# One tile distance in each stage, and w_out tiles split two units ahead, in an fp32 hybrid encoder layer

## The chip, the cores and the metric

The kernel runs on one core of a Trainium2 chip. The metric is the time of one execution on the device in microseconds, as the median of several runs. The chip's engines that matter here are PE (TensorE: matmuls, and the loads of their stationary operand), DVE (VectorE), ACT (ScalarE), POOL (GpSimd) and SP (SyncE, which here only issues DMAs).

## The reference

One encoder layer on x of 256 positions by 2048 channels, batch 1, everything in float32:

```python
xn = _rmsnorm(h, pre_mix_gain[l])
proj = xn @ w_in[l]                       # 2048 x 3904: hyena x0, x1, v | latents of the attention
xh = _dwconv_centred(xh, hyena_conv_w[l], hyena_conv_b[l])
y_hyena = x0 * _bidir_long_conv(x1 * v, k2, hyena_bias[l])
y_attn = _mla(c_q, c_kv, k_pe, ...)       # 8 heads, softmax over 256 keys
mixed = concatenate([_rmsnorm(y_hyena), _rmsnorm(y_attn)]) @ w_out[l]     # 2048 x 2048
h = h + _rmsnorm(mixed, post_mix_gain[l])
hn = _rmsnorm(h, pre_ffn_gain[l])
gu = hn @ w_up[l]                         # 2048 x 11264
g = _dwconv_centred(gu[..., :D_FF], ffn_conv_w[l], ffn_conv_b[l])
f = (gelu(g) * gu[..., D_FF:]) @ w_down[l]    # 5632 x 2048
h = h + _rmsnorm(f, post_ffn_gain[l])
```

## The kernel before

Every weight is read once from memory, in units of 128 x 1024 floats (512 KB). `load` (L131) issues the DMA on SP's queue into a `raw` tile. `split_w` makes two tiles of it: a high part `wh`, a cast to the rounded format fp32r on ACT (L140), and a low part `wl`, the rest, as a subtraction on DVE (L143). `raw`, `wh` and `wl` come from the pool `wp` with four buffers each, so a unit's load waits until the unit four before it has been split, and a split waits until PE is done with the unit four before. The activations are split in the same way. PE then multiplies high by high, high by low and low by high.

PE's stages, in the order of the program:

- The input's norm and the attention's latents.
- The hyena projection: 24 half outputs `hi` of two units each (`why...`, L113 to L115, three matmuls of 256 columns for each of 16 k). The weights are the stationary operand, the activations `xT` move. Attention and the long convolution run between them as generators in the list `chains`; `turn()` takes each one step further after every unit. `hyena_tail` finishes a half output: `z` (L616), then the three taps of the convolution (`cv`, L551 and L553).
- The output projection (`wo`, L100 to L102): `row_units` runs over two halves of 16 units (`w_out00` to `w_out015`, `w_out10` to `w_out115`). Here the activations `mix[k]` are stationary and the weights move, 512 columns at a time; a unit is 12 matmuls (two row blocks, two column blocks, three products). `row_units` stages one unit ahead of the one that PE uses. During the first eight units the last steps of the chains still run: `channel_norm` scales and splits `ya` and `yh` into `mix` on DVE (L763 and L92), with the row scale spread over partitions by a matmul (`rbh`, L161). The rest of the row vectors follow: `gbm` and `gbn` (two gain vectors, spread over 128 partitions, 1 MB each) and `h` (x, two loads of 1 MB) are loaded through POOL's queue (L873 to L877).
- Norms and the first tile of the up projection, whose weights have a pool of their own (`up0`).
- The up projection (`pg` and `pu`, `wmm`, L108 and L109): 43 more tiles of four units each. The weights are stationary. For each of 16 k, and for `pg` and `pu`, one matmul of 512 columns with the high weights and one of 256 columns with the low weights, a pair; 32 pairs a tile. `up_tail` makes the gated result `fT[n]`.
- The down projection (`wd`, also L100 to L102): two halves of 44 units, `fT[k]` stationary, weights moving; then the last norm and the output.

PE loads the stationary operand of the next matmul while the present one runs. Where the two tiles lie in SBUF is set by the pools: `W_SLOT = 1024 + 16` floats makes each of the four slots of `wh` and `wl` begin 64 bytes further than the last, counted modulo 256 bytes, so that the four units in use begin at 0, 64, 128 and 192. `xT` and `hnT` begin at 0, `mix` at 128; `fT` has a pad of 16 floats after every four tiles, so that it steps by 64 bytes too. The order of the work on each engine is that of the code, except where `tc.issue_after` puts an instruction behind a named one.

Of the kernel before, what the change touches and what calls it, by code (L numbers as in the profile page):

```python
# [12 lines left out]
F32 = mybir.dt.float32  # L13
F32R = mybir.dt.float32r
# [4 lines left out]
P = 128  # L19
D = 2048  # L20
S = 256
KD = D // P
# [6 lines left out]
NF = DFF // P  # L29
# [20 lines left out]
V_FCB = 274  # L50
V_ALL = 318
V_PAD = 320
W_SLOT = 1024 + 16


def _body(ctx, tc, a):
    nc = tc.nc
# [6 lines left out]

    const = ctx.enter_context(tc.tile_pool(name="const", bufs=1))
    edge = ctx.enter_context(tc.tile_pool(name="edge", bufs=1, side="right"))
    edge.tile([P, 24], F32, name="edge")
    wp = ctx.enter_context(tc.tile_pool(name="wp", bufs=4))
    psA = ctx.enter_context(tc.tile_pool(name="psA", bufs=2, space=bass.MemoryType.PSUM))
    psB = ctx.enter_context(tc.tile_pool(name="psB", bufs=3, space=bass.MemoryType.PSUM))  # L70
# [59 lines left out]

    def load(src, n, name):  # L131
        raw = wp.tile([P, 1024], F32, tag="raw", name=name)
        nc.sync.dma_start(raw[:, :n], src)
        return raw

    def split_w(raw, n, name, pool=None, cut=None):
        pool = pool or wp
        h = pool.tile([P, W_SLOT], F32R, tag="wh", name=name + "h")
        l = pool.tile([P, W_SLOT], F32R, tag="wl", name=name + "l")
        box["cast"] = nc.scalar.copy(h[:, :n], raw[:, :n])  # L140
        for e, o in ((nc.vector, slice(0, cut or n)), (nc.gpsimd, slice(cut or n, n))):
            if o.start < n:
                box["lo"] = e.tensor_tensor(l[:, o], raw[:, o], h[:, o].bitcast(F32), op=ALU.subtract)  # L143
        return h, l

    def stage(src, n, name, pool=None, cut=None):

        return split_w(load(src, n, name), n, name, pool, cut)

    def rms_scale(ss, n, name, pool, bufs=4):  # L150
        v = small(pool, 1, tag="rv", name=name + "v", bufs=bufs)
# [14 lines left out]
    box = {}  # L166
# [13 lines left out]
    yp = l_stack.enter_context(tc.tile_pool(name="yp", bufs=1, side="left"))  # L180
    spec = l_stack.enter_context(tc.tile_pool(name="spec", bufs=1, side="left"))
    xTp = l_stack.enter_context(tc.tile_pool(name="xTp", bufs=1, side="left"))
    xT = [xTp.tile([P, 2, 2, P], F32R, name=f"xT{k}") for k in range(KD)]
    ya = [yp.tile([P, S], F32, name=f"ya{i}") for i in range(8)]
    yh = [yp.tile([P, S], F32, name=f"yh{i}") for i in range(8)]
# [15 lines left out]
    x = a["x"]  # L201
# [114 lines left out]
    for k in range(KD):  # L316
# [7 lines left out]
        wh, wl = wm[k]  # L324
# [445 lines left out]
    def attention_chain():  # L770
        nonlocal mixp, mix
        yield from latents()
        yield from attention()
        yield from pause(2)
        at_stack.close()
        mixp = mix_stack.enter_context(tc.tile_pool(name="mixp", bufs=1, side="right"))
        mix = [mixp.tile([P, 2, S], F32R, name=f"mix{k}") for k in range(KD)]
        yield from channel_norm(sqa, ya, V_AG, mix[0:8], "a", mi)

    mixp = mix = None  # L780
# [3 lines left out]
    next(att)  # L784
    order = [(0, 0), (0, 1), (1, 0), (0, 2), (1, 1), (2, 0),
             (2, 1), (1, 2), (3, 0), (3, 1), (2, 2), (3, 2)]
    for i, gi in order:
        for c in range(2):
            ps = (acc if cv else mj)(f"hi{i}{gi}{c}")[:, :S]
            for kh in range(2):  # L790
                wh, wl = stage(a["w_hy"][i, gi, c, kh], 1024, f"why{i}{gi}{c}{kh}")
                for kk in range(8):
                    k = kh * 8 + kk
                    wm3(ps, wh[:, kk * P : (kk + 1) * P], wl[:, kk * P : (kk + 1) * P], xT[k],
                        k == 0, k == KD - 1)
                if kh == 1:
                    if not cv:
                        row_scale_tile()
                    hyena_tail(i, gi, c, ps)
                turn()  # L800

    def row_units(wname, nk, half, lT, ps, hold, held):
        def get(k):
            return stage(a[wname][half, k], 1024, f"{wname}{half}{k}")

        nxt = get(0)
        for k in range(nk):
            w, nxt = nxt, get(k + 1) if k + 1 < nk else None
            for b in range(2):
                if b == 1 and k >= nk - hold:  # L810
                    held.append((k, w))
                    continue
                for c in range(2):
                    row_emit(ps[b][c], lT, k, b, w, c, nk)
            yield
# [35 lines left out]
        return rms_scale(ss, n, nm, pool)  # L851

    psw = row_banks(0, "wo0")
    units = row_units("w_out", KD, 0, mix, psw, 0, None)
    for _ in range(8):
        next(units)
        turn()
# [5 lines left out]
    h = [hp.tile([P, D], F32, name=f"h{b}") for b in range(2)]  # L863
    rb2 = hp.tile([P, S], F32, name="rb2")
    hn_stack = es()
    hnp = hn_stack.enter_context(tc.tile_pool(name="hnp", bufs=1, side="left"))
    hnTq = [hnp.tile([P, 4, 2, 2, P], F32R, name=f"hnT{c}") for c in range(4)]
    hnT = [hnTq[k // 4][:, k % 4] for k in range(KD)]
    pm_stack = es()
    pm = pm_stack.enter_context(tc.tile_pool(name="pm", bufs=1, side="left"))  # L870
    up0 = pm_stack.enter_context(tc.tile_pool(name="up0", bufs=4, side="left"))
    gbm = pm.tile([P, D], F32, name="gbm")
    nc.gpsimd.dma_start(gbm, a["post_mix_gain"].partition_broadcast(P))  # L873
    gbn = pm.tile([P, D], F32, name="gbn")
    nc.gpsimd.dma_start(gbn, a["pre_ffn_gain"].partition_broadcast(P))
    for b in range(2):
        nc.gpsimd.dma_start(h[b], x[b * P : (b + 1) * P, :])  # L877
    tmp = [pm.tile([P, D], F32, name=f"tmp{b}") for b in range(2)]
    ssq = [small(pm, 4, name=f"ssq{b}") for b in range(2)]
    ss2 = [small(pm, 4, name=f"ss2{b}") for b in range(2)]  # L880
    for _ in units:
        pass
    for b in range(2):
        for c in range(2):
            row_finish(psw, 0, b, c, gbm, tmp, ssq, pm)
# [26 lines left out]
    held = []  # L912
    psw = row_banks(1, "wo1")
    for k, _ in enumerate(row_units("w_out", KD, 1, mix, psw, HOLD, held)):
        if k == KD - HOLD - 2:
            first = [stage(a["w_up"][0, kq], 1024, f"wup0{kq}", up0) for kq in range(4)]
    row_finish(psw, 1, 0, 0, gbm, tmp, ssq, pm)
# [12 lines left out]
    fq = fpa_stack.enter_context(tc.tile_pool(name="fq", bufs=2, side="right"))  # L930
    fpa = fpa_stack.enter_context(tc.tile_pool(name="fpa", bufs=1, side="right"))
    NFA = 12
    def gated_tiles(pool, ks):
        for k in ks:
            if k % 4 == 0:
                pool.tile([P, 16], F32, name=f"fpad{k}")
            yield pool.tile([P, 2, S], F32R, name=f"fT{k}")

    fT = list(gated_tiles(fpa, range(NFA)))

    def up_tail(n, pg, pu):

# [49 lines left out]
    for n in range(1, NF):  # L992
        if n == 4:
            fpb = fpa_stack.enter_context(tc.tile_pool(name="fpb", bufs=1, side="right"))
            fT += gated_tiles(fpb, range(NFA, NF))
        new = (mi, mj) if n % 2 else (acc, acc)
        pg, pu = as4(new[0](f"pg{n}")), as4(new[1](f"pu{n}"))
        chs = []
        for kq in range(4):
            with es() as hold:  # L1000
                if n == 1:
                    for eng in range(2):
                        hold.enter_context(tc.issue_after(box[int(kq >= 2), 3, eng].ins))
                chs.append(stage(a["w_up"][n, kq], 1024, f"wup{n}{kq}"))
        for which, ps in ((0, pg), (1, pu)):
            for k in range(KD):
                wh, wl = chs[k // 4]
                o = (k % 4) * 256 + which * P
                wmm(ps, wh[:, o : o + P], wl[:, o : o + P], hnT[k], k == 0, k == KD - 1)
        up_tail(n, pg, pu)  # L1010
# [16 lines left out]
    for half in range(2):  # L1027
        psd = row_banks(half, f"wd{half}")
        held = []
# [117 lines left out]
```

## Time and profile before

| | |
|---|---|
| time, median of 3 runs | 1115.65 us (1114.95 to 1116.01) |
| the profiled execution | 1114.86 us |
| its span | 1113.1 us |
| PE busy | 1096.4 us, 99% |
| DVE, ACT, POOL busy | 65%, 52%, 11% |
| hyena projection, attention, long convolution | about 46 to 259 us |
| output projection | 259 to 352 us |
| norms, first tile of the up projection | 352 to 378 us |
| up projection, 43 tiles | 378 to 860 us |
| down projection | 860 to 1098 us |

The span is the time from the first to the last instruction of the profiled execution; some 2 us lie around it. PE's share of 99% says how long matmuls were running, not how fast they followed one another: the timeline of single matmuls tells that, from the start of one to the start of the next (a matmul's own duration there is longer than the spacing, since matmuls are pipelined). The mean of a group is taken from two rows far apart and the count of matmuls between them.

### The profile page before, as it was taken

To read this page: it belongs to the slowest core of one execution; us is meant where nothing else is said; L and a number is where in the kernel's file an instruction comes from. 1 tells how busy PE (TensorE), PEld (TensorE's weight loads), DVE (VectorE), ACT (ScalarE), POOL (GpSimd) and SP (SyncE) were. 2 spreads that over 40 slices of the span, in tenths; PEclk is the share of its full clock that TensorE was granted. 3 is DMA by queue.
4 is the path that set the end of the run, shared out by engine and by line. 5 is a ranking of instruction groups with operands and counts; after the bars stand their busy time and mean duration, and the time that the engine had idled before them with its cause. 6 is when DMAs were issued, how large, how long until landed. Compare 5 with 4: busy or idle time off the path is not lost.

```text
span 1113.1 us, 16496 instructions
## 1 busy us (share of the span) xinstructions
PE 1096.4 (99%) x6334; PEld 959.4 (86%) x6334; DVE 725.8 (65%) x1051; ACT 574.3 (52%) x884; POOL 122.3 (11%) x154
## 2 busy tenths in 40 slices
PE   9999999999999999999999999999999999999997
PEld 7899999998787888888888888888888888888885
DVE  7898878889567766666666666565756444454444
ACT  7756656655454646454545455554545333343332
POOL 4300100011002311111111111111111000000000
PEclk9999999999999999999999999999999999999999
DMA  9664445444775354645464645555555766666652
GB/s 312 224 212 148 161 133 171 143 136 131 276 253 189 114 190 162 216 157 219 156 214 164 204 176 197 182 188 191 179 199 172 258 188 191 189 192 188 189 191 95
DMA packets 59207, 207.23 MB, mean 186 GB/s; under 512 B 6903, under 2 KB 7801, under 8 KB 58489
## 3 DMA queue, kind: packets, MB, share of 16 engines
q1 hardware_dynamic: 57832, 200.39, 54.1%
q0 software_dynamic: 720, 5.24, 1.3%
q8 instruction: 49, 0.80, 0.3%
q10 hardware_dynamic: 576, 0.56, 0.1%
q14 instruction: 30, 0.24, 0.1%
HBM read 204.07 MB, written 2.10 MB: 185 GB/s over the span
## 4 chain that ended last, share of the span: by engine, by line
PE 86%; issue 6%; DVE 5%; DMA 1%; POOL 1%; ACT 1%; DVEq 0%; POOLq 0%; SPq 0%; ACTq 0%
PE pg L108 14%; PE pu L108 14%; PE pg L109 7%; PE pu L109 7%; PE wd L102 7%; PE wd L100 7%; PE wd L101 7%; PE hi L113 4%; PE hi L115 4%; PE hi L114 4%; DMA w_out<-in_w_out 1%; POOL tmp L893 1%; PE y L499 1%; PE pq L101 1%; PE pq L100 1%
## 5 line engine op out<-in xcount | busy, mean ns | idle before, releaser
L91 ACT CAST fT<-u 128x256 fp32r<-128x256 f32 x44 | 17.8, 406 | 111.1 <-DVE u L952 111.0
L551 DVE SCALAR_TENSOR_TENSOR t<-g,vec,t 128x255 f32<-128x255 f32 x44 | 21.3, 483 | 63.8 <-ACT t L550 63.8
L948 POOL TENSOR_TENSOR u<-u,rb 128x256 f32<-128x256 f32 x44 | 32.4, 736 | 276.4 <-DVE u L125 276.4
L550 ACT ACTIVATE t<-g,vec 128x256 f32<-128x256 f32 x44 | 26.5, 603 | 54.9 <-POOL g L946 54.9
L125 DVE TENSOR_TENSOR g<-pg,jg 128x256 f32<-128x256 f32 x44 | 18.7, 424 | 52.5 <-ACT jg L124 52.5
L946 POOL TENSOR_TENSOR g<-g,rb 128x256 f32<-128x256 f32 x44 | 32.4, 736 | 137.6 <-DVE g L125 136.2
L124 ACT COPY jg<-pg 128x256 f32<-128x256 f32 x44 | 16.3, 371 | 54.7 <-PE pg L109 54.7
L952 DVE TENSOR_TENSOR u<-u,t 128x256 f32<-128x256 f32 x44 | 18.7, 424 | 36.4 <-POOL u L948 35.4
L834 POOL TENSOR_TENSOR rw0r<-rw0v,neghalf 128x1 f32<-128x1 f32 x2 | 1.1, 558 | 292.1 <-DVE rw0v L831 292.1
L92 DVE TENSOR_TENSOR fT<-u,fT 128x256 fp32r<-128x256 f32 x44 | 18.7, 425 | 19.8 <-ACT fT L91 19.8
L553 DVE SCALAR_TENSOR_TENSOR t<-g,vec,t 128x255 f32<-128x255 f32 x44 | 21.3, 484 | 1.5
L547 POOL TENSOR_TENSOR sqa<-sqa,sqa 128x256 f32<-128x256 f32 x7 | 6.8, 965 | 128.9 <-ACT sqa L546 128.6
L951 ACT ACTIVATE t<-t 128x256 f32<-128x256 f32 x44 | 18.2, 414 | 2.7 <-DVE t L553 2.7
L125 DVE TENSOR_TENSOR u<-pu,ju 128x256 f32<-128x256 f32 x44 | 18.3, 417 | 0.0
L550 ACT ACTIVATE cv<-z,vec 128x256 f32<-128x256 f32 x24 | 14.4, 601 | 7.5 <-DVE z L616 7.5
L232 POOL TENSOR_TENSOR sqx<-sqx,sqx 128x256 f32<-128x256 f32 x15 | 15.7, 1047 | 17.8 <-ACT sqx L231 17.6
L124 ACT COPY ju<-pu 128x256 f32<-128x256 f32 x44 | 16.0, 364 | 0.0
L96 DVE SCALAR_TENSOR_TENSOR xT<-xraw,vec,xT 128x256 fp32r<-128x256 f32 x16 | 11.8, 740 | 2.7 <-ACT xT L95 2.7
L893 POOL TENSOR_TENSOR tmp<-h,gbn 128x512 f32<-128x512 f32 x8 | 13.3, 1682 | 2.4 <-DVE h L890 2.4
L616 DVE TENSOR_TENSOR z<-hi,rbx 128x256 f32<-128x256 f32 x24 | 10.0, 418 | 5.2 <-PE hi L115 4.9
L547 POOL TENSOR_TENSOR sqh<-sqh,sqh 128x256 f32<-128x256 f32 x7 | 7.8, 1114 | 47.6 <-ACT sqh L546 47.5
L553 DVE SCALAR_TENSOR_TENSOR cv<-z,vec,cv 128x255 f32<-128x255 f32 x24 | 12.4, 518 | 0.2
(3679 smaller groups left out, 4378.0 us busy)
## 6 DMA issues: line engine op xcount, KB each, us to landing
wup<-in_w_up SPq DMA_DIRECT2D x176, 512.0 KB, 4.8
w_down<-in_w_down SPq DMA_DIRECT2D x88, 512.0 KB, 3.5
why<-in_w_hy SPq DMA_DIRECT2D x48, 512.0 KB, 3.9
w_out<-in_w_out SPq DMA_DIRECT2D x32, 512.0 KB, 4.3
wm<-in_w_mla SPq DMA_DIRECT2D x16, 416.0 KB, 4.9
win<-in_window SPq DMA_DIRECT2D x8, 256.0 KB, 3.1
wuq<-in_w_uqn SPq DMA_DIRECT2D x4, 512.0 KB, 3.5
wkv<-in_w_ukv SPq DMA_DIRECT2D x4, 512.0 KB, 4.1
```

The source lines that it names most:

```text
L100: ins = nc.tensor.matmul(ps, lhsT=lh, rhs=rh, start=first, stop=False)
L101: nc.tensor.matmul(ps, lhsT=lh, rhs=rl, start=False, stop=False)
L102: nc.tensor.matmul(ps, lhsT=ll, rhs=rh, start=False, stop=last)
L108: nc.tensor.matmul(ps, lhsT=wh, rhs=xt, start=first, stop=False)
L109: nc.tensor.matmul(ps[:, :, 0, :], lhsT=wl, rhs=xt[:, :, 0, :], start=False, stop=last)
L113: nc.tensor.matmul(ps, lhsT=wh, rhs=xt[:, :, 0, :], start=first, stop=False)
L114: nc.tensor.matmul(ps, lhsT=wh, rhs=xt[:, :, 1, :], start=False, stop=False)
L115: box["mm"] = nc.tensor.matmul(ps, lhsT=wl, rhs=xt[:, :, 0, :], start=False, stop=last)
L125: nc.vector.tensor_add(d, ps4[:, :, 0, :], lo)
L550: nc.scalar.activation(dst, src, AF.Identity, bias=vc(bv), scale=vc(wv + 1))
L553: nc.vector.scalar_tensor_tensor(dst[:, : S - 1], src[:, 1:], vc(wv + 2), dst[:, : S - 1], op0=ALU.mult, op1=ALU.add)
L946: nc.gpsimd.tensor_tensor(g, g, rb2, op=ALU.mult)
```

## The change

There are three parts.

1. The layout. `W_SLOT` goes: all four slots of `wh` and of `wl` begin at the same place modulo 256 bytes. `wl` gets 64 floats more, so that a low tile can be put `o` floats further; the up projection's 43 tiles use `o=16`, 64 bytes. New pads move `xT` and `hnT` to 64 and `mix` to 0; the pads within `fT` go and it lies at 0. The address of the stationary tile less that of the moving one, modulo 256, becomes 192 in the hyena projection, 0 in the output and down projections, and in the up projection 192 for the high and 0 for the low weights. Before, it ran through 0, 64, 128 and 192 in each of them.
2. `row_units` keeps two units staged ahead, and the first two units of `w_out` are staged in the last half output of the hyena projection (`got`).
3. `gbm`, `h` and `gbn` are no longer loaded in four pieces of 1 MB through POOL's queue; twelve pieces go through SP's, each behind the load of one unit (`piece`): four of `gbm` behind `w_out010` to `w_out013`, four of `h` (512 KB) behind `w_out11` to `w_out14`, four of `gbn` behind `w_out15` to `w_out18`.

```diff
-W_SLOT = 1024 + 16
-    edge.tile([P, 24], F32, name="edge")
+    edge.tile([P, 40], F32, name="edge")
...
-        nc.sync.dma_start(raw[:, :n], src)
+        box["load"] = nc.sync.dma_start(raw[:, :n], src)
...
-    def split_w(raw, n, name, pool=None, cut=None):
+    def split_w(raw, n, name, pool=None, cut=None, o=0):
+
         pool = pool or wp
-        h = pool.tile([P, W_SLOT], F32R, tag="wh", name=name + "h")
-        l = pool.tile([P, W_SLOT], F32R, tag="wl", name=name + "l")
+        h = pool.tile([P, 1024], F32R, tag="wh", name=name + "h")
+        l = pool.tile([P, 1024 + 64], F32R, tag="wl", name=name + "l")[:, o : o + 1024]
...
+    xTp.tile([P, 16], F32, name="xpad")
     xT = [xTp.tile([P, 2, 2, P], F32R, name=f"xT{k}") for k in range(KD)]
...
         mix = [mixp.tile([P, 2, S], F32R, name=f"mix{k}") for k in range(KD)]
+        mixp.tile([P, 16], F32, name="mpad")
...
+    got = []
     for i, gi in order:
...
+                if (i, gi, c) == (3, 2, 1):
+                    got.append(stage(a["w_out"][0, kh], 1024, f"w_out0{kh}"))
...
-    def row_units(wname, nk, half, lT, ps, hold, held):
+    def row_units(wname, nk, half, lT, ps, hold, held, got=()):
...
-        nxt = get(0)
+        ws = list(got) or [get(0)]
         for k in range(nk):
-            w, nxt = nxt, get(k + 1) if k + 1 < nk else None
+            if len(ws) < nk:
+                ws.append(get(len(ws)))
+            w = ws[k]
...
+    hnp.tile([P, 16], F32, name="hpad")
...
-    nc.gpsimd.dma_start(gbm, a["post_mix_gain"].partition_broadcast(P))
...
-    nc.gpsimd.dma_start(gbn, a["pre_ffn_gain"].partition_broadcast(P))
-    for b in range(2):
-        nc.gpsimd.dma_start(h[b], x[b * P : (b + 1) * P, :])
+
+    def piece(dst, src, c, n):
+
+        o = slice(c * n, (c + 1) * n)
+        with tc.issue_after(box["load"].ins):
+            nc.sync.dma_start(dst[:, o], src[:, o])
+
...
-    for _ in units:
-        pass
+    for k, _ in enumerate(units):
+        if k < 4:
+            piece(gbm, a["post_mix_gain"].partition_broadcast(P), k, 512)
...
+        if k < 4:
+            piece(h[k // 2], x[k // 2 * P : (k // 2 + 1) * P, :], k % 2, 1024)
+        elif k < 8:
+            piece(gbn, a["pre_ffn_gain"].partition_broadcast(P), k - 4, 512)
...
-    def gated_tiles(pool, ks):
-        for k in ks:
-            if k % 4 == 0:
-                pool.tile([P, 16], F32, name=f"fpad{k}")
-            yield pool.tile([P, 2, S], F32R, name=f"fT{k}")
-
-    fT = list(gated_tiles(fpa, range(NFA)))
+    fT = [fpa.tile([P, 2, S], F32R, name=f"fT{k}") for k in range(NFA)]
+    fpa.tile([P, 16], F32, name="fpad")
...
-                chs.append(stage(a["w_up"][n, kq], 1024, f"wup{n}{kq}"))
+                chs.append(stage(a["w_up"][n, kq], 1024, f"wup{n}{kq}", o=16))
```

What stands on DVE at the end of the hyena projection, before. `z321` and `cv321` are the last half output's tail, `ya` and `mix` the attention's part of the output projection's stationary operand, `w_out01l` the low part of the second unit:

```order
L616 TENSOR_TENSOR z321_3587<-hi321_3520,rbx_125 128x256
L763 SCALAR_TENSOR_TENSOR ya4_111<-ya4_111,vec_74,rba_3238 128x256
L763 SCALAR_TENSOR_TENSOR ya5_112<-ya5_112,vec_74,rba_3238 128x256
L551 SCALAR_TENSOR_TENSOR cv321_3589<-z321_3587,vec_74,cv321_3589 128x255
L92 TENSOR_TENSOR mix4_3226<-ya4_111,mix4_3226 128x256
L553 SCALAR_TENSOR_TENSOR cv321_3589<-z321_3587,vec_74,cv321_3589 128x255
L92 TENSOR_TENSOR mix5_3227<-ya5_112,mix5_3227 128x256
L143 TENSOR_TENSOR w_out01l_3612<-w_out01_3609,w_out01h_3611 128x1024
L763 SCALAR_TENSOR_TENSOR ya6_113<-ya6_113,vec_74,rba_3238 128x256
L763 SCALAR_TENSOR_TENSOR ya7_114<-ya7_114,vec_74,rba_3238 128x256
L143 TENSOR_TENSOR w_out02l_3651<-w_out02_3648,w_out02h_3650 128x1024
```

The same place on DVE in the changed kernel:

```order
L143 TENSOR_TENSOR w_out01l_3598<-w_out01_3595,w_out01h_3597 128x1024
L617 TENSOR_TENSOR z321_3601<-hi321_3522,rbx_126 128x256
L764 SCALAR_TENSOR_TENSOR ya4_112<-ya4_112,vec_74,rba_3240 128x256
L764 SCALAR_TENSOR_TENSOR ya5_113<-ya5_113,vec_74,rba_3240 128x256
L552 SCALAR_TENSOR_TENSOR cv321_3603<-z321_3601,vec_74,cv321_3603 128x255
L91 TENSOR_TENSOR mix4_3227<-ya4_112,mix4_3227 128x256
L554 SCALAR_TENSOR_TENSOR cv321_3603<-z321_3601,vec_74,cv321_3603 128x255
L143 TENSOR_TENSOR w_out02l_3620<-w_out02_3617,w_out02h_3619 128x1024
L91 TENSOR_TENSOR mix5_3228<-ya5_113,mix5_3228 128x256
L764 SCALAR_TENSOR_TENSOR ya6_114<-ya6_114,vec_74,rba_3240 128x256
L764 SCALAR_TENSOR_TENSOR ya7_115<-ya7_115,vec_74,rba_3240 128x256
```

`w_out01l` now stands ahead of `z321`, and `w_out02l` ahead of `mix5`.

SP's queue in the second part of the first half of `w_out`, before (`w_out09` to `w_out014` are the units' loads):

```order
L133 DMA w_out09_3866<-in_w_out 128x1024
L133 DMA w_out010_3884<-in_w_out 128x1024
L133 DMA w_out011_3902<-in_w_out 128x1024
L133 DMA w_out012_3920<-in_w_out 128x1024
L133 DMA w_out013_3938<-in_w_out 128x1024
L133 DMA w_out014_3956<-in_w_out 128x1024
```

And in the changed kernel:

```order
L132 DMA w_out09_3821<-in_w_out 128x1024
L132 DMA w_out010_3871<-in_w_out 128x1024
L887 DMA gbm_3863<-in_post_mix_gain 128x512
L132 DMA w_out011_3890<-in_w_out 128x1024
L887 DMA gbm_3863<-in_post_mix_gain 128x512
L132 DMA w_out012_3909<-in_w_out 128x1024
L887 DMA gbm_3863<-in_post_mix_gain 128x512
L132 DMA w_out013_3928<-in_w_out 128x1024
L887 DMA gbm_3863<-in_post_mix_gain 128x512
L132 DMA w_out014_3947<-in_w_out 128x1024
```

The four quarters of `gbm`, which was one issue on POOL, stand each behind one unit's load.

## Rows read from the trace of the kernel before

**Rows 1.** The page's busy time of each engine, share of the span, instructions.

```profile
PE 1096.4 (99%) x6334; PEld 959.4 (86%) x6334; DVE 725.8 (65%) x1051; ACT 574.3 (52%) x884; POOL 122.3 (11%) x154
```

**Rows 2.** Timeline of PE, hyena projection: start, duration, line, operation, tiles, shapes.

```profile
204.19 0.28 PE L113 MATMUL hi<-xT,why3001h 128*128 128x256 f32 x1
...
206.89 0.28 PE L115 MATMUL hi<-xT,why3001l 128*128 128x256 f32 x1
...
209.88 0.28 PE L113 MATMUL hi<-xT,why3010h 128*128 128x256 f32 x1
...
212.76 0.28 PE L113 MATMUL hi<-xT,why3011h 128*128 128x256 f32 x1
...
215.37 0.28 PE L115 MATMUL hi<-xT,why3011l 128*128 128x256 f32 x1
```

**Rows 3.** Windows: length; busy of PE, PEld, DVE, ACT, POOL; clock; DMA share; GB/s.

```profile
204.00:216.00 12.00, 12.00 (x104) 12.00 (x104) 10.31 (x21) 8.66 (x19) 1.48 (x2) 1.00 0.44 136
265.00:270.00 5.00, 3.23 (x8) 2.62 (x9) 5.00 (x9) 1.35 (x3) 0.00 (x0) 0.71 0.37 105
300.00:310.00 10.00, 10.00 (x45) 8.11 (x44) 2.43 (x3) 2.30 (x3) 0.00 (x0) 1.00 0.99 385
```

**Rows 4.** Timeline of PE, two units of the output projection.

```profile
323.82 0.39 PE L102 MATMUL wo<-w_out14h,mix 128*128 128x512 f32 x1
...
325.40 0.39 PE L100 MATMUL wo<-w_out15h,mix 128*128 128x512 f32 x1
...
326.80 0.39 PE L100 MATMUL wo<-w_out15h,mix 128*128 128x512 f32 x1
```

**Rows 5.** Timeline of PE, down projection: first matmuls of units 0 and 39, second half.

```profile
982.67 0.39 PE L100 MATMUL wd<-w_down10h,fT 128*128 128x512 f32 x1
...
1090.94 0.39 PE L100 MATMUL wd<-w_down139h,fT 128*128 128x512 f32 x1
```

**Rows 6.** Timeline of PE, up projection, tile 22 and the start of tile 23.

```profile
612.67 0.39 PE L108 MATMUL pg<-hnT,wup220h 128*128 128x512 f32 x1
...
615.48 0.40 PE L108 MATMUL pg<-hnT,wup222h 128*128 128x512 f32 x1
...
616.53 0.40 PE L108 MATMUL pg<-hnT,wup222h 128*128 128x512 f32 x1
...
616.90 0.39 PE L108 MATMUL pg<-hnT,wup223h 128*128 128x512 f32 x1
...
623.93 0.39 PE L108 MATMUL pg<-hnT,wup230h 128*128 128x512 f32 x1
```

**Rows 7.** Timeline of PE, start of the output projection; in brackets idle before, releaser.

```profile
259.00 0.39 PE L100 MATMUL wo<-w_out00h,mix 128*128 128x512 f32 x1
...
266.77 0.56 PE L101 MATMUL wo<-w_out01l,mix 128*128 128x512 f32 x1 [1.84 <-DVE w_out01l L143]
...
267.55 0.63 PE L101 MATMUL wo<-w_out01l,mix 128*128 128x512 f32 x1
267.98 0.63 PE L102 MATMUL wo<-w_out01h,mix 128*128 128x512 f32 x1
...
285.62 0.92 PE L161 MATMUL rbh<-dgnh,ones 128*128 128x128 f32 x4 [0.81 <-DVE dgnh L160]
...
292.14 0.39 PE L100 MATMUL wo<-w_out09h,mix 128*128 128x512 f32 x1
```

**Rows 8.** Timeline of DVE, ACT and POOL in the same stretch.

```profile
265.50 1.22 DVE L143 TENSOR_TENSOR w_out01l<-w_out,w_out01h 128x1024 fp32r<-128x1024 f32 x1
...
282.13 1.05 ACT L140 CAST w_out08h<-w_out 128x1024 fp32r<-128x1024 f32 x1 [5.02 <-DMA w_out<-in_w_out]
...
295.70 1.12 POOL L877 DMA_DIRECT2D h<-in_x  x2 [10.04 <-DVE mix L92]
```

**Rows 9.** DMA issues: transfer, queue, count, KB each, median us to landing.

```profile
gbm<-in_post_mix_gain POOLq DMA_DIRECT2D x1, 1024.0 KB, 9.2
...
h<-in_x POOLq DMA_DIRECT2D x2, 1024.0 KB, 10.6
```

More of the change, by code (lines that the diff above doesn't have):

```diff
@@ L144, in split_w, with stage @@
         return h, l
-    def stage(src, n, name, pool=None, cut=None):
-        return split_w(load(src, n, name), n, name, pool, cut)
+    def stage(src, n, name, pool=None, cut=None, o=0):
+        return split_w(load(src, n, name), n, name, pool, cut, o)
     def rms_scale(ss, n, name, pool, bufs=4):
@@ L853, in _body @@
     psw = row_banks(0, "wo0")
-    units = row_units("w_out", KD, 0, mix, psw, 0, None)
+    units = row_units("w_out", KD, 0, mix, psw, 0, None, got)
     for _ in range(8):
@@ L994, in _body @@
             fpb = fpa_stack.enter_context(tc.tile_pool(name="fpb", bufs=1, side="right"))
-            fT += gated_tiles(fpb, range(NFA, NF))
+            fT += [fpb.tile([P, 2, S], F32R, name=f"fT{k}") for k in range(NFA, NF)]
         new = (mi, mj) if n % 2 else (acc, acc)
```

## The prediction

> **What bounds the kernel now.** I read the page's engine line first: PE is busy 99% of the span, DVE and ACT far less [rows 1]. So only two things can move the end: work that PE does not have, or the time between the starts of two matmuls. The page cannot show the second, since an engine that is always busy looks the same at any pace, so I went to the timeline of PE and divided the time between two starts by the matmuls between them. In the hyena projection the same 256-column matmul comes every 2.70/23 = 117.4 ns in one half tile, 2.88/24 = 120.0 in the next, 2.61/23 = 113.5 in the one after [rows 2]. These half tiles have the same shapes, the same moving tiles and a granted clock of 1.00 [rows 3]; what changes is which of the four weight slots they read, and a slot lies 64 bytes further than its neighbour, counted modulo 256. I call *distance* the address of the stationary tile, which PE loads beside the running matmul, minus that of the moving tile, modulo 256 bytes: it was 64, 0 and 192 in those three. In the output projection, 512 columns, two neighbouring units show the same thing: 7 spacings in 1.58 us at distance 0 (225.7 ns), then 6 in 1.40 at distance 64 (233.3) [rows 4]. The rows are rounded to 10 ns, so the first is known to some 1.5 ns. Over whole passes, where all four distances take turns: the down projection needs 108.27 us for 39 units of 12 matmuls, 231.3 ns each [rows 5], and a tile of the up projection 11.26 us for its 32 pairs of one 512- and one 256-column matmul, 352 ns a pair [rows 6]. Last I looked for places where PE does have to wait; the one cluster is the start of the output projection [rows 7, 8].
>
> **The change part by part.**
>
> *Down projection.* All units go to distance 0. Each matmul gains 231.3 - 226.7 = 4.6 ns; I take 226.7, the upper part of what 1.58/7 allows, because the first matmuls after a change of distance are longer. The code has 2 x 44 units x 12 = 1056 matmuls: **-4.9 us**. All of it lies on the path, because the next unit's weights are there already (DVE is busy 65% of the span, ACT 52% [rows 1]). Bounds: 0 if the distance 0 does not stay locked, -5.9 with 225.7.
>
> *Output projection, pace.* The same for some 370 matmuls outside the starting trouble: 370 x 4.6 = **-1.7 us** (0 to -2.1).
>
> *Output projection, start.* In the trace PE waits 1.84 us for the low part of the second unit, w_out01l, which DVE made only at 265.50, and then runs eight matmuls at a spacing of 0.43 us instead of 0.23 (267.55 to 267.98 [rows 7]): 8 x 0.2 = 1.6 us more. The granted clock of 265 to 270 is 0.71 [rows 3], a mean over full speed (2.4 GHz) and the half of it, after PE had stood still. Eighteen us later the row-scale broadcast waits 0.81 us behind DVE [rows 7]: DVE had stood behind w_out08l, whose cast had waited 5.02 us for its DMA [rows 8]. While that DMA was late, a 1 MB load of a gain vector, 9.2 us to landing, went through the POOL queue beside it [rows 9]. The order of DVE shows w_out01l ahead of z321 and w_out02l where w_out01l was; the two casts and subtractions (1.05 and 1.22 us each [rows 8]) move into the last half tiles of the hyena projection, where PE has its own work. The 1 MB loads leave the POOL queue. So 1.84 + 1.6 + 0.81 = **-4.3 us**. What is late next: z321 now stands 1.22 us further back, and with it the chain to the broadcast, so part of the 0.81 can return; and mix5 to mix7 slip behind two low parts, but they are wanted by units 5 to 7, some 14 us after the first unit. Bounds: -2.0 (the wait is gone, but a shorter one and the slow matmuls stay) to -5.5 (smaller gaps of the same stretch, 33.14 us from w_out00 to w_out09 of which 9 x 12 matmuls are 25.0 [rows 7], close too).
>
> *The loads on SP's queue.* The 4 MB come as 12 pieces, each behind one weight unit. A unit lasts PE 12 x 0.2267 = 2.72 us. At 385 GB/s, what the stretch 300 to 310 moved with the DMA engines 0.99 busy [rows 3], 512 KB take 1.36 us; a unit with a 512 KB piece is 2.72, with a 256 KB piece 2.04. So it just fits, with a lead of about three units in the raw buffers. Behind a piece on SP stand all later weight loads; a piece whose buffer is not free holds them up. For h that can happen: on POOL its load waited until DVE was done with the hyena rows, at 295.70 [rows 8]. The lead of 8 us covers that. I take 0; bounds 0 to the rival below.
>
> *Hyena projection.* One distance, 192, for all half tiles. The rows at 192 give 113.5, but only after a half tile at 0; at 64 the row is 117.4, about the mean of the three (117.0) [rows 2]. About 1150 matmuls: from -4.5 (113.5 everywhere) to +0.5. I take 0, since gaps and transposes break the pattern often and the commoner value then comes back.
>
> *Up projection.* The largest and least certain term: 43 tiles x 32 = 1376 pairs, so 1 ns a pair is 1.38 us. While the 512-column matmul runs, PE loads the low weights (now distance 0), while the 256-column one runs, the next high weights (distance 192). From below: both settle as in the other stages, 225.7 + 113.5 = 339. Against it: within this stage the four pairs at distance 0 took 1.42 us, 355 each [rows 6]; but there the distance changed every four pairs, and now the pattern stays for all 43 tiles. I take the middle of the two, 348: 1376 x -4 ns = **-5.5 us**, bounds -17.9 and +4.1.
>
> *A rule that speaks against all of the layout terms.* The same matmul at 120.0, 117.4 and 113.5 ns [rows 2] says that weight loads and moving reads get in each other's way by address. The Trainium skill ("TensorE: Matmul & The Clock Gate", section "Step-by-step: what each phase is for") says the opposite: TensorE has two independent read ports, and "Loading the next tile's weights doesn't steal SBUF read bandwidth from the running matmul." By that rule the layout would be worth nothing; it is rival D.
>
> Sum: -4.9 - 1.7 - 4.3 + 0 + 0 - 5.5 = **-16.4 us**. The profiled execution took 1114.86 us beside the median's 1115.65, near enough to take the difference off the median: 1099.3.
>
> **The rivals.** *B, the up projection keeps the 355 ns of its own rows:* +4.1 in place of -5.5: 1115.65 - 10.9 + 4.1 = 1108.9. For it: it is the only row at distance 0 in this stage. Against: those four pairs include the change of distance. *C, everything locks fast:* 339 in the up projection gives 1086.9, and with 113.5 in the hyena projection 1082.4. For it: both shapes have been seen at these spacings; against: never in alternation. *D, the address does nothing:* spacing differences would come from something that goes with the slots, and only the start is won: 1115.65 - 4.3 = 1111.4. Against it stand [rows 2, 4]. *E, SP's queue gets late:* if a 256 KB piece costs a quarter of the 9.2 us of a gain's 1 MB [rows 9], 2.3, a unit with one takes 2.3 + 1.36, 0.94 more than PE's 2.72; eight such are 7.5 us, and four 512 KB pieces of h at 2.65 (10.6 for the two loads of 1 MB that ran together [rows 9]) add 5.2. Less the lead of 8.2 that is 4.5 late, plus one fall of the clock, 1.6: 1105.4; without any lead 12.7 + 1.6 = 14.3 late, 1113.6. For it: those landings were measured in this very stretch. Against: they shared the DMA engines with three to four weight loads. *S, slower: the up projection locks in a slow pattern.* One pair at distance 0 took 0.37 us, 616.53 to 616.90 [rows 6]. If the constant distance repeats that pair for ever, 1376 x 18 ns = +24.8 us: 1115.65 - 10.9 + 24.8 = 1129.5. It decides from a pair of 360 ns on (10.9/1376 = 7.9 ns above 352), and is measurably slower from 361.5.
>
> **How the numbers follow.** A measurement of this kernel tells 0.2%, 2.2 us, from no change. Forecast with a pair of 343 to 353 (1092 to 1106): 0.54; C 0.16; B 0.13; E 0.08, half of it within 0.2%; D 0.03; S 0.06. Faster: 0.54 + 0.16 + 0.13 + 0.04 + 0.03 = 0.90, same 0.04, slower 0.06. The range from 1087 to 1111 leaves out S, the slow half of E, and the fastest part of C, together some 0.15.
>
> **What would show it.** A tile of the up projection (11.26 us before) should take 11.1; 11.4 is B, 10.85 is C, 11.8 is S. A w_down unit should take 2.72 us instead of 2.775 and the units should not differ; if they still differ in groups of four, D is right. PE should start w_out01 without a wait, and the granted clock at 260 to 275 should stay at 1.00. ACT's casts of w_out09 to w_out19 should wait less than 5 us on DMA; longer waits with PE idle behind them are E. The hyena half tiles should all show one spacing, 113 or 117 to 118. I am wrong if the time is outside the range, and wrong in the reason if the time fits but the down projection's pace has not changed.

## The result, and the profile after

The changed kernel takes 1085.26 us (median of 4 runs, 1084.86 to 1087.20) beside 1115.30 for the kernel before: a ratio of 0.9734, with an interval of 0.9717 to 0.9751. That is 30 us saved where 16.4 were forecast, 1.7 us below the low end of the range. The page's engine line (busy time, share, instructions):

```profile
PE 1069.9 (99%) x6334; PEld 947.9 (87%) x6334; DVE 726.3 (67%) x1051; ACT 570.5 (53%) x884; POOL 122.0 (11%) x150
```

PE has as many instructions as before [rows 1] and the same share of the span, and is busy 26.5 us less: nearly all of the gain is pace. To see where, I took the first matmul of each stage from the timeline of PE (start, duration, line, tiles). Before, where [rows 5, 7] don't give it:

```profile
358.40 0.39 PE L963 MATMUL pg<-hnT,wup00h 128*128 128x256 f32 x1 [0.44 <-DVE hnT L900]
...
860.53 0.39 PE L100 MATMUL wd<-w_down00h,fT 128*128 128x512 f32 x1
...
1104.58 0.40 PE L102 MATMUL wd<-w_down143h,fT 128*128 128x512 f32 x1
```

and after, with the unit w_out09 and the broadcast of [rows 7], the tile of [rows 6] and the units of [rows 5]:

```profile
257.19 0.39 PE L99 MATMUL wo<-w_out00h,mix 128*128 128x512 f32 x1
...
279.39 0.61 PE L161 MATMUL rbh<-dgnh,ones 128*128 128x128 f32 x4
...
285.29 0.39 PE L99 MATMUL wo<-w_out09h,mix 128*128 128x512 f32 x1
...
350.20 0.39 PE L974 MATMUL pg<-hnT,wup00h 128*128 128x256 f32 x1 [0.42 <-DVE hnT L912]
...
596.93 0.39 PE L107 MATMUL pg<-hnT,wup220h 128*128 128x512 f32 x1
...
607.82 0.39 PE L107 MATMUL pg<-hnT,wup230h 128*128 128x512 f32 x1
...
836.29 0.39 PE L99 MATMUL wd<-w_down00h,fT 128*128 128x512 f32 x1
...
956.00 0.39 PE L99 MATMUL wd<-w_down10h,fT 128*128 128x512 f32 x1
...
1062.08 0.39 PE L99 MATMUL wd<-w_down139h,fT 128*128 128x512 f32 x1
...
1075.45 0.39 PE L101 MATMUL wd<-w_down143h,fT 128*128 128x512 f32 x1
```

| stretch | before | after | difference | forecast |
|---|---|---|---|---|
| start to first w_out matmul | 259.00 | 257.19 | -1.8 | 0 |
| first w_out to first up matmul | 99.40 | 93.01 | -6.4 | -6.0 |
| up projection, first tile included | 502.13 | 486.09 | -16.0 | -5.5 |
| down projection, first to last matmul | 244.05 | 239.16 | -4.9 | -4.9 |
| rest | 8.52 | 8.15 | -0.4 | 0 |

The tile of the up projection takes 10.89 us, 340.3 ns a pair instead of 352, and the down projection 106.08/468 = 226.7 ns a matmul instead of 231.3. At the start of the output projection both waits are gone: w_out01 and the broadcast have no idle time before them, and from w_out00 to w_out09 it is 28.10 us instead of 33.14. The window that had a granted clock of 0.71 [rows 3] (length; busy of PE, PEld, DVE, ACT, POOL; clock; DMA share; GB/s):

```profile
265.00:270.00 5.00, 5.00 (x23) 4.14 (x23) 5.00 (x10) 2.67 (x5) 0.00 (x0) 1.00 0.48 142
```

and the longest wait of an ACT cast for a w_out DMA in the stage (engine, line, releaser: us, times, longest), where w_out08h had waited 5.02 us [rows 8]:

```profile
ACT w_out09h L140 <- DMA w_out<-in_w_out: 2.4, 1, 2.4
```

In the hyena projection, now all at distance 192, two paces are left:

```profile
175.97 0.28 PE L112 MATMUL hi<-xT,why2111h 128*128 128x256 f32 x1
...
178.09 0.28 PE L112 MATMUL hi<-xT,why2111h 128*128 128x256 f32 x1
...
180.80 0.28 PE L112 MATMUL hi<-xT,why1200h 128*128 128x256 f32 x1
...
183.52 0.28 PE L112 MATMUL hi<-xT,why1201h 128*128 128x256 f32 x1
```

18 spacings in 2.12 us are 117.8 ns, 24 in 2.72 are 113.3: same line, same addresses modulo 256, 3 us apart. Of the 48 half tiles 35 have no gap in them; counted over PE's timeline, 16 of these take 113 ns and 19 take 118, where before 11 took 113, 13 took 117 to 119 and 11 took 120. That was the first hint of what the experiments showed.

### The profile page after: what moved, and what is told of

It is laid out like the page before. It is cut to its first block, busy times and chain, and to the rows that moved or that the text cites. A ratio compares the mean times of both kernels' runs of the same rounds, so it can differ in the third digit from the quotient of the medians.

```text
span 1083.6 us, 16504 instructions
## 1 busy us (share of the span) xinstructions
PE 1069.9 (99%) x6334; PEld 947.9 (87%) x6334; DVE 726.3 (67%) x1051; ACT 570.5 (53%) x884; POOL 122.0 (11%) x150
## 4 chain that ended last, share of the span: by engine, by line
PE 92%; DVE 4%; issue 2%; ACT 1%; POOL 1%; DMA 0%; DVEq 0%; POOLq 0%; SPq 0%; ACTq 0%
PE pu L107 14%; PE pg L107 14%; PE wd L100 7%; PE wd L101 7%; PE wd L99 7%; PE pu L108 7%; PE pg L108 7%; PE hi L113 4%; PE hi L112 4%; PE hi L114 4%; PE wo L99 2%; PE wo L101 2%; PE wo L100 2%; PE pq L100 1%; PE y L500 1%
```

## The experiments

Three theories; the two numbers in brackets are the distances of the high and of the low weights, so the changed up projection runs at (192, 0). **Theory 1:** the distance alone sets the spacing, each pair of distances having its own. **Theory 2:** any distances that stay settle at the best pace, and before the changes cost the time. **Theory 3:** at given distances there are several paces that hold themselves, and how a stretch is entered picks one.

**The layout alone** (staging and POOL's loads as before):

```diff
-                if (i, gi, c) == (3, 2, 1):
-                    got.append(stage(a["w_out"][0, kh], 1024, f"w_out0{kh}"))
...
+        nxt = get(0)
+            w, nxt = nxt, get(k + 1) if k + 1 < nk else None
...
+    nc.gpsimd.dma_start(gbm, a["post_mix_gain"].partition_broadcast(P))
```

> The new layout alone: w_out is staged one unit ahead again and the gain vectors and h go through POOL's queue in 1 MB loads, as before. If the parts add up, this is 1085.3 plus the start of the output projection, 4.3 us: 1089.6, a ratio of 0.977 to before; PE waits about 1.8 us for w_out01l again, and the up projection's pair stays at 340 ns. If the layout's gain in the output projection (w_out tiles come faster than DVE can split them) needs the earlier staging, it is 1092 or more. A rival says that the order and the layout do not matter separately, since the pace of the pairs is won by having no late weights: then the pair goes back towards 352 and the time towards 1105.

1091.98 us, ratio 0.9793 (0.9771 to 0.9816): near the higher of the values I had given, and PE waits 1.83 us for w_out01 again. The five executions were 1089.5, 1090.7, 1092.0, 1092.4 and 1105.8, and the profiled one is the 1105.8. Its PE timeline, first matmuls of tiles 22 and 23:

```profile
610.03 0.40 PE L107 MATMUL pg<-hnT,wup220h 128*128 128x512 f32 x1
...
621.23 0.40 PE L107 MATMUL pg<-hnT,wup230h 128*128 128x512 f32 x1
```

11.20 us, 350 ns a pair at the addresses that gave 340.3. Over 43 tiles, 1376 x 9.7 ns = 13.3 us, about what this execution is above the others. Addresses alone do not set the pace.

**The staging alone** (old layout, w_out two ahead, pieces on SP): the diff of the change without its lines on `W_SLOT`, pads and `o`.

> The old layout with w_out two units ahead and the twelve pieces on SP's queue. My sum gave 4.3 us for this: 1111.0, ratio 0.996. The up and down projections must show the old paces, 352 ns a pair and 231.3 ns a matmul. If the staging were the source of more than that (the unexpected 14 us), 1100.

1110.88 us, ratio 0.9966 (0.9956 to 0.9976), as expected. Its tile 22:

```profile
608.87 0.40 PE L108 MATMUL pg<-hnT,wup220h 128*128 128x512 f32 x1
...
620.16 0.40 PE L108 MATMUL pg<-hnT,wup230h 128*128 128x512 f32 x1
```

11.29 us, the old pace (353). So 26 us of the gain need the layout.

**Both weights of the up projection at 192:**

```diff
-                chs.append(stage(a["w_up"][n, kq], 1024, f"wup{n}{kq}", o=16))
+                chs.append(stage(a["w_up"][n, kq], 1024, f"wup{n}{kq}"))
```

> The changed kernel, but in the up projection the low weights lie 64 bytes nearer again, so that high and low weights have both distance 192. Theory 1 (the pair of distances sets the pace; 0 under the 512-column matmul is what steers the pair to 340 ns): the pair is slower, 229 + 117.8 = 347 ns by the settled values of the two shapes, +9 us: 1094.5. Theory 2 (any pair of distances that does not change settles at the fast pace; what cost time before was the change every four pairs): 340 ns again, 1085.3.

1099.99 us, ratio 0.9872 (0.9843 to 0.9902). Tile 22:

```profile
602.52 0.39 PE L107 MATMUL pg<-hnT,wup220h 128*128 128x512 f32 x1
...
613.68 0.40 PE L107 MATMUL pg<-hnT,wup230h 128*128 128x512 f32 x1
```

11.16 us, 349 ns. The four executions fall into two pairs, 1097.3 and 1097.8, 1102.2 and 1103.2; only the first was profiled. The distance is constant here and the pace is not 340: theory 2 falls. The 64 bytes more for the low weights are worth 12 us against the better pair.

**Low weights at 64, and the down projection at 64:** `o=32` in both projections, and no `fpad`.

> The changed kernel with the low weights 128 bytes on (distance 64) in the up projection and in the hyena projection, and fT moved so that the down projection runs at distance 64 throughout. Theory 1: the down projection takes 233 ns a matmul, the value seen at 64 before, +6.5 us; the pair of the up projection is slower than 340. Theory 2: the down projection settles at 226.7 and the pair at 340, since nothing changes within either stage; the time stays at 1085. The hyena projection shows whether a low part at another distance than the high part takes its two paces, 113 and 118 ns, to one.

1111.21 us, one execution. Tile 22, and the two units of [rows 5]:

```profile
606.28 0.40 PE L107 MATMUL pg<-hnT,wup220h 128*128 128x512 f32 x1
...
617.59 0.40 PE L107 MATMUL pg<-hnT,wup230h 128*128 128x512 f32 x1
...
978.23 0.39 PE L99 MATMUL wd<-w_down10h,fT 128*128 128x512 f32 x1
...
1087.42 0.39 PE L99 MATMUL wd<-w_down139h,fT 128*128 128x512 f32 x1
```

11.31 us, 353 ns a pair, and 109.19/468 = 233.3 ns in the down projection: what two units of [rows 4] had shown, now for a whole pass. Theory 2 falls again, and so does the rival that addresses do nothing. The hyena projection with its low weights at 64 keeps two paces: 17 half tiles of the 35 take 113 ns, the others 118 to 119.

**The changed kernel once more:**

> The changed kernel once more, unaltered. In the profiled execution of the layout alone, all tiles of the up projection from the third on took 350 ns a pair at the same addresses that gave 340 in the changed kernel, and the other four executions were 14 us faster. Theory 3: at one pair of distances there are two paces that hold themselves, and how the stage is entered picks one for all of it. Then some of these executions may be some 14 us slower (1099), if the changed kernel too can fall into the slow pace. Theory 1 (the addresses alone decide): all executions at 1085.

1085.97 us; six executions: 1084.5, 1084.9, 1085.6, 1086.4, 1098.4, 1098.6. The same program has two times, 13 us apart. So the changed kernel, too, falls to the 350 ns in some executions. The two long ones were not profiled; that their pairs take 350 ns is argued from the layout's profile and the size. Their granted clock, 0.999 and 0.997, is that of the other four.

**Both at 0, and the two distances exchanged** (`hpad` left out, with `o` at 0 or 48 in the up projection; 16 in the hyena projection of the first, 48 and no `xpad` there in the second):

> The changed kernel with distance 0 for both the high and the low weights of the up projection, and the low weights of the hyena projection at distance 0 beside high ones at 192. If the distance under which a matmul runs sets its spacing as in the stages with one distance, the pair is 226.7 + 120.0 = 346.7 ns, +9 us: 1094. If 0 under the 512-column matmul is enough, 340. In the hyena projection the low part at 0 may steer all half tiles to 113 ns, as it does in the up projection (-4 us), or give two matmuls at 113 to 118 and one at 120 (+1 us).

> The two distances of the up projection the other way round: high weights at 0, low weights at 192; the same in the hyena projection. If it matters which load runs under which matmul, the pair is 229 + 120 = 349 ns, +12 us: 1097; if only the mixture of 0 and 192 matters, 340. In the hyena projection 120 under two of three matmuls would be +1 us, steering to 113 would be -4 us.

1105.64 and 1102.59 us, one execution each. Tile 22 of the first and of the second kernel:

```profile
607.72 0.40 PE L107 MATMUL pg<-hnT,wup220h 128*128 128x512 f32 x1
...
619.02 0.40 PE L107 MATMUL pg<-hnT,wup230h 128*128 128x512 f32 x1
```

```profile
606.26 0.40 PE L107 MATMUL pg<-hnT,wup220h 128*128 128x512 f32 x1
...
617.50 0.39 PE L107 MATMUL pg<-hnT,wup230h 128*128 128x512 f32 x1
```

353 and 351 ns, where adding the spacings of the two shapes gave 346.7 and 349. A pair's pace is not the sum of what its matmuls take elsewhere. In the hyena projection, mixing 0 and 192 led to the slower pace: all of the 35 half tiles without a gap took 118 ns, where the changed kernel has 16 at 113.

**The changed kernel with gains and h on POOL's queue again:**

```diff
+    nc.gpsimd.dma_start(gbm, a["post_mix_gain"].partition_broadcast(P))
+    nc.gpsimd.dma_start(gbn, a["pre_ffn_gain"].partition_broadcast(P))
...
-            piece(gbm, a["post_mix_gain"].partition_broadcast(P), k, 512)
```

> The changed kernel with the gain vectors and h loaded through POOL's queue in 1 MB loads again; w_out still two units ahead. If the 1 MB loads beside the weight loads were what made w_out08 late, PE waits again near the broadcast, some 0.8 to 2.5 us with the fall of the clock: 1086 to 1088. If two units ahead cover that, 1085.3, and the pieces are worth nothing.

1091.78 us (0.9788, 0.9771 to 0.9805), 6 us more than the changed kernel, where I had expected 1 to 3. Timelines of PE and ACT, and a window:

```profile
284.12 1.22 PE L161 MATMUL rbh<-dgnh,ones 128*128 128x128 f32 x4 [4.60 <-DVE dgnh L160]
```

```profile
280.65 1.04 ACT L140 CAST w_out09h<-w_out 128x1024 fp32r<-128x1024 f32 x1 [5.91 <-DMA w_out<-in_w_out]
```

```profile
285.00:290.00 5.00, 5.00 (x14) 3.95 (x14) 3.85 (x8) 1.95 (x4) 0.00 (x0) 0.52 0.68 230
```

The cast of w_out09 waits 5.91 us for its DMA while the DMA engines are 0.97 busy (280 to 285 us), the broadcast behind it on DVE makes PE idle 4.60 us, and then PE has half of its clock (0.52, the level of 1.2 GHz) for some 5 us. So splitting two ahead moves the first wait away, but the late DMA then strikes PE harder. The pieces on SP's queue are what takes it away; whether their size or their queue does it was not separated. The parts do not add up either (the layout's other four executions have a median of 1091.3; the staging saves 4.0): the staging is worth some 6 us on the new layout and 4 on the old. Of the 2 us between, the staging alone loses 1.1 in the up projection (353 for 352 ns a pair). For the rest one profile each speaks: in the layout alone the broadcast waits 1.62 us and the granted clock of 285 to 290 is 0.66, where before it waits 0.81 and the clock stays at 1.00. That the faster w_out units are why the 1 MB loads cost more there is argued, not shown.

**Two k of the hyena projection at 0, to steer the rest:**

```diff
-    xTp.tile([P, 16], F32, name="xpad")
-    xT = [xTp.tile([P, 2, 2, P], F32R, name=f"xT{k}") for k in range(KD)]
+    xT = [xTp.tile([P, 2, 2, P], F32R, name=f"xT{k}") for k in range(2)]
+    xTp.tile([P, 16], F32, name="xpad")
+    xT += [xTp.tile([P, 2, 2, P], F32R, name=f"xT{k}") for k in range(2, KD)]
```

> The changed kernel, but the activations of the first two k of the hyena projection lie 64 bytes nearer, so that the first six matmuls of each half output run at distance 0 and the other 42 at 192. In the kernel before, a half tile at 192 took 113.3 ns a matmul whenever it came right after one at 0, and 113 or 118 otherwise. Theory 3 (two paces hold themselves, the entry picks one): 6 x 120 and 42 x 113.3, a mean of 114.1 instead of 117.0 ns, about 1130 matmuls: -3.3 us, 1082. Theory 1 (addresses alone): 192 has its pace whatever comes before, 117 and a little for the six at 120: +0.4 us, 1085.7.

1086.01 us: no gain. Matmuls 7 and 22 of a half tile:

```profile
120.90 0.28 PE L112 MATMUL hi<-xT,why1100h 128*128 128x256 f32 x1
...
122.67 0.28 PE L112 MATMUL hi<-xT,why1100h 128*128 128x256 f32 x1
```

The 15 spacings behind the six at 0 take 1.77 us, 118.0 ns, not 113. Of the 35 half tiles without a gap only 2 take 113, where the changed kernel has 16: a few matmuls at 0 lead to the slower pace, the opposite of what I expected. Nor does 113 need a half tile at 0 ahead of it, as [rows 2] had made me think, since the changed kernel has none at 0. I have no rule for what gives it. One of the four executions took 1100.8.

**Low weights in turn at 0, 192, 0, 64, 0, 128, tile by tile** (and one k of the hyena projection at 0):

```diff
-                chs.append(stage(a["w_up"][n, kq], 1024, f"wup{n}{kq}", o=16))
+                chs.append(stage(a["w_up"][n, kq], 1024, f"wup{n}{kq}", o=(16, 0, 16, 32, 16, 48)[(n - 1) % 6]))
```

> The changed kernel with low weights of the up projection at distance 0 in every other tile and at 192, 64 and 128 in turn in the tiles between; in the hyena projection one k of 16 at distance 0. Theory 3: each tile at (192, 0) enters anew and picks 340 or 350 ns a pair for all its 32 pairs; which one may depend on the tile before. Theory 1: all the tiles at (192, 0) take 340. The tiles between take 349 at 192 and 353 at 64; 128 is unknown. With 340 in half of the tiles the time is 1085.3 + 21 tiles x 32 x 11 ns = 1093; with 350 in all of them 1100. One k at distance 0 (three matmuls) steers the hyena projection as two do, or is too short.

1094.57 us, one execution. First matmuls of tiles 3 to 14:

```profile
391.22 0.39 PE L107 MATMUL pg<-hnT,wup30h 128*128 128x512 f32 x1
...
402.42 0.40 PE L107 MATMUL pg<-hnT,wup40h 128*128 128x512 f32 x1
...
413.72 0.39 PE L107 MATMUL pg<-hnT,wup50h 128*128 128x512 f32 x1
...
424.60 0.40 PE L107 MATMUL pg<-hnT,wup60h 128*128 128x512 f32 x1
...
435.70 0.39 PE L107 MATMUL pg<-hnT,wup70h 128*128 128x512 f32 x1
...
446.60 0.39 PE L107 MATMUL pg<-hnT,wup80h 128*128 128x512 f32 x1
...
457.89 0.40 PE L107 MATMUL pg<-hnT,wup90h 128*128 128x512 f32 x1
...
468.79 0.39 PE L107 MATMUL pg<-hnT,wup100h 128*128 128x512 f32 x1
...
479.88 0.40 PE L107 MATMUL pg<-hnT,wup110h 128*128 128x512 f32 x1
...
491.08 0.39 PE L107 MATMUL pg<-hnT,wup120h 128*128 128x512 f32 x1
...
502.18 0.39 PE L107 MATMUL pg<-hnT,wup130h 128*128 128x512 f32 x1
...
513.07 0.39 PE L107 MATMUL pg<-hnT,wup140h 128*128 128x512 f32 x1
```

| tile | low weights at | us | ns a pair |
|---|---|---|---|
| 3 | 0 | 11.20 | 350 |
| 4 | 64 | 11.30 | 353 |
| 5 | 0 | 10.88 | 340 |
| 6 | 128 | 11.10 | 347 |
| 7 | 0 | 10.90 | 341 |
| 8 | 192 | 11.29 | 353 |
| 9 | 0 | 10.90 | 341 |
| 10 | 64 | 11.09 | 347 |
| 11 | 0 | 11.20 | 350 |
| 12 | 128 | 11.10 | 347 |
| 13 | 0 | 10.89 | 340 |

Tiles 3, 5, 7, 9, 11 and 13 have the same addresses. From tile 7 on, such a tile takes 340 after one at 192 or 128 and 350 after the one at 64, and this repeats every six tiles to the end of the stage. That is theory 3, and the choice is not chance. But the tile before does not make it alone: tile 3, behind one at 192 (which also holds the disturbance described in the last section), took 350, and tile 5, behind one at 64, took 340. The tile at 64 led from 350 to 340 there and from 340 to 350 the six times after, so what it leaves depends on the pace that it meets, and it takes 353 in the first case and 347 in the others. The tile at 128 led to 340 from either pace (tiles 6 and 12).

**Switching on purpose:**

```diff
-                chs.append(stage(a["w_up"][n, kq], 1024, f"wup{n}{kq}", o=16))
+                chs.append(stage(a["w_up"][n, kq], 1024, f"wup{n}{kq}", o={10: 32, 26: 48}.get(n, 16)))
```

> The changed kernel, but of the 43 tiles of the up projection tile 10 has its low weights at distance 64 and tile 26 at 128; all others stay at (192, 0). In the alternating kernel a tile at 64, entered from 340, was followed by one at 350, and a tile at 128 by one at 340, every time. Theory 3, if a pace once picked holds: 340 ns a pair up to tile 9, 346 in tile 10, 350 in tiles 11 to 25, 346 in tile 26 and 340 from tile 27 on; time 1085.3 + 15 tiles x 32 x 10 ns = 4.8 us and 0.4 for the two tiles: 1090.5. Theory 1 (addresses alone): 340 in all but the two tiles, 1085.8. If the tiles before 10 come in at 350, then tile 10 turns them to 340 (so it was with tiles 3 to 5 of the alternating kernel).

1091.39 us (one execution), expected 1090.5. First matmuls of tiles 9 to 11 and 26 to 28:

```profile
456.21 0.39 PE L107 MATMUL pg<-hnT,wup90h 128*128 128x512 f32 x1
...
467.09 0.39 PE L107 MATMUL pg<-hnT,wup100h 128*128 128x512 f32 x1
...
478.18 0.40 PE L107 MATMUL pg<-hnT,wup110h 128*128 128x512 f32 x1
...
646.18 0.39 PE L107 MATMUL pg<-hnT,wup260h 128*128 128x512 f32 x1
...
657.28 0.39 PE L107 MATMUL pg<-hnT,wup270h 128*128 128x512 f32 x1
...
668.17 0.39 PE L107 MATMUL pg<-hnT,wup280h 128*128 128x512 f32 x1
```

10.88 us in tile 9, 11.09 in tile 10, then 168.00 for the 15 tiles from 11 to 25, 11.20 each, 11.10 in tile 26, and 10.89 again in tile 27. One tile switches the pace, and it holds for 15 tiles until another switches it back.

**Steering once, in tile 3:** `o=48 if n == 3 else 16`.

> The changed kernel with the low weights of tile 3 alone at distance 128. In the alternating kernel a tile at 128 was followed by 340 whether 340 or 350 came before it. Theory 3: tile 3 costs 32 x 6.5 ns = 0.2 us, and every execution runs the tiles from 4 on at 340: a median of 1085.5, and none of the executions near 1099, of which the changed kernel had two in six. Theory 1 says the same of the median; if executions near 1099 are left, what is picked there is not picked before tile 3, or something else makes them slow.

1085.74 us (1085.28 to 1086.94, five executions), ratio 0.9743 (0.9725 to 0.9761): the changed kernel's time, as expected, with no execution near 1099. Of the other kernels with the pair (192, 0) in all tiles, 4 executions of 23 were 13 to 15 us longer, so five without one is weak evidence by itself; what speaks for the edit is that a tile at 128 led to 340 from both sides above. The profiled execution does not show the steering: its tile 2 already ended at 340 ns a pair. No version was faster than the changed kernel by more than the measurement tells.

## Why the prediction was wrong

**The step that failed** is the term of the up projection: "I take the middle of the two, 348". It measured 340.3 ns and -16.0 us in place of -5.5, 10.5 of the 13.6 us that were missing. The lower end, 339, was there as the sum of two settled spacings. The upper, 355, came from four pairs [rows 6] whose high and low weights both lie at 0, since the slots of both step alike; the change puts the high weights at 192. It was a row of another pair of distances, and not much in error for that one: held for a whole stage, (0, 0) takes 353. So the 355 was no bound for (192, 0), and neither was the 0.37 us of rival S, a pair of the same row. The middle of the two was also 347, not 348, which would have been -6.9 us and still far off. But 339 was not right for the reason I gave either: the same sum fails for (0, 0), 346.7 against 353, so that it came near here is luck. What the stage does is to hold one of several paces, 340 or 350 at these distances, and most executions hold the better.

**The hyena projection** was put at 0 within -4.5 to +0.5, and the stretch up to w_out gained 1.8: 16 half tiles in place of 11 of the 35 without a gap come to 113 ns, and none of them is left at 120. (From the mean of 117.0 the lower bound should have been -4.0.) The commoner value did not simply come back, as I had argued; which half tiles take 113 is open. This term moved the time from the edge of the range, the 1086.9 of rival C, to below it. I had cut the range short of C's lower half although C's two parts were both at hand in the rows.

**The down projection** is right in mechanism and size: 226.7 ns, -4.9 us. **The output projection** too: -6.4 for -6.0, the wait, the slow matmuls and the wait before the broadcast all gone. Its inner split was off: I gave the loads only the 0.81 us of the broadcast's wait, and without the pieces the new layout loses 6 us.

**The rivals.** *D* (addresses do nothing) is refuted by the staging alone, which keeps 353 ns and saves only 4 us, by the 12 us that 64 bytes in the place of the low weights are worth, and by 226.7 against 233.3 ns in the down projection when in that stage nothing but fT's place differs. By the Trainium skill's sentence on the read ports ("TensorE: Matmul & The Clock Gate", section "Step-by-step: what each phase is for") the place would cost nothing; here the spacing changes with it, and the measurement decides. Whether the weight load takes read bandwidth from the matmul, no run here shows. *E* (SP's queue late): no; the casts wait at most 2.4 us for their loads and PE waits for no w_out unit. *S* named a real thing, a slow pace that holds itself, but with 370 ns from one pair; it is 350, and still faster than before. *B*'s 355 is near what other pairs of distances take, 349 to 353, and its own pair, (0, 0), above all, but not this one.

## What to carry to other kernels

Where PE is 99% busy, divide start to start by the number of matmuls: here the same shape differed by 3% (226.7 and 233.3 ns) to 6% (113.3 and 120.0), and the modulo-256 addresses of stationary and moving tile are a cheap thing to try, both for the high and the low weights. When a row is to price a stage, check that both weight tiles of a pair have in that row the distances that the stage will give them. Measure each pair over a whole stage, since spacings of other stages don't add up, and look at several executions, since a pace can hold for a whole stage and be picked at its start. And look at large loads beside a stream of weight loads when the units get faster: here cutting 1 MB loads into pieces on the stream's own queue was worth 6 us.

## What the runs showed of the hardware that I had not expected

At one pair of distances (192 for the high, 0 for the low weights) a pair of matmuls takes 340 or 350 ns, at (192, 64) 347 or 353; a stretch keeps its pace for 15 tiles (168 us) and more, and one tile at another distance can switch it. Which way a tile at 64 switches it depends on the pace that it meets: from 340 to 350 seven times in the two kernels that tried, from 350 to 340 once. What picks the pace in the ordinary kernel is open. In all seven traces whose tiles 1 and 2 are at (192, 0), the 13th pair of tile 2 takes 0.62 to 0.70 us, without a wait in the record. In the profiled execution of the layout alone (first pair of tile 2, 13th and 14th):

```profile
385.88 0.39 PE L107 MATMUL pg<-hnT,wup20h 128*128 128x512 f32 x1
...
389.96 0.39 PE L107 MATMUL pg<-hnT,wup23h 128*128 128x512 f32 x1
...
390.58 0.39 PE L107 MATMUL pg<-hnT,wup23h 128*128 128x512 f32 x1
```

The 12 pairs of the tile before that place took 4.08 us, 340 ns each, and those behind it 350, to the end of the stage: here the pace changed within the stage, and at that place. In the other six traces it is 339 to 340 before and 340 to 342 in the rest of the tile. What the disturbance is, and why it led to 350 in one of the seven, was not tried. Nor did a run move both tiles of a matmul by the same amount: that their difference counts and not the place of either is argued, from 225.7 ns at distance 0 with `mix` at 128 [rows 4] and 226.7 with `fT` at 0. Why a distance matters at all, the traces do not say.
